# The mixers of block 1: mLSTM gate rows broadcast through DRAM, its scores as three products of two alternating heads, and k norms taken from the transposed k

## The chip, the core and the metric

The kernel runs on one core of a Trainium2 chip. The core has a matrix engine (TensorE, in the profile PE, with its weight loads as PEld), a vector engine (VectorE, DVE), a scalar engine (ScalarE, ACT), a general engine (GpSimd, POOL) and queues that start DMA transfers (one is SyncE's, SP; GpSimd and ScalarE have their own). Each engine takes its instructions in the order in which they stand in its queue, and a wait of the first holds all behind it. The metric is the device time of one execution in microseconds (us), as a median over runs.

## The reference

The program is a two-block transformer in float32 with one sequence of T = 512 rows and a width of 1024. The change lies in the two recurrent mixers of block 1. Both have H = 4 heads. What they compute, cut to what matters here:

```python
# gated delta rule: q, k, v after a causal convolution of width 4 and silu, heads of 128
q = _l2norm(q) * (dk ** -0.5)          # _l2norm(x) = x * rsqrt(sum(x*x, -1) + 1e-6)
k = _l2norm(k)
# mLSTM: q, k with 64 per head, v with 128; b = running sum of log sigmoid(f_pre)
d_log = where(incl, b[..., :, None] - b[..., None, :] + i[..., None, :], -inf)
s = einsum('bhcd,bhsd->bhcs', q_i, k_i) * exp(d_log - m_t[..., None])
num = ... + einsum('bhcs,bhse->bhce', s, v_i)
den = ... + sum(s, axis=-1)
h = num / maximum(abs(den), exp(-m_t))[..., None]
```

The kernel computes the mLSTM in one piece over all 512 rows: per head a triangle of scores between key block j and all later queries, each score times the exponential of a row term (one number a query, the same for all keys of a block) plus a column term.

## The kernel before

**The large products.** Nearly all of the work is products of a weight slab (1024x128) with the 512 columns of the activations. A slab is loaded by SP (raw, 512 KB), cast to its leading part by ACT (`whi`, line 101), and the rest is subtracted by DVE (`wlo`, line 102). Then PE multiplies three times for each of 8 pieces: 24 matmuls of 128x512 in the reduced format fp32r, lines 173 to 175.

**Who sets the order.** PE's order in block 1 is written out by hand. The slab products stand in a list, `todo`, cut into steps of six matmuls (four steps a slab). The code of the mixers is written between calls of `fill(n)`, which issue n such steps. A slab that is done may hand work over for later: `after(n, fn)` runs `fn` once n more steps are issued.

```python
def after(n, fn):
    late.append((now[0] + n, fn))
def fill(n):
    for _ in range(n):
        run_late(now[0])
        now[0] += 1
        while todo and next(todo[0], 1):
            todo.pop(0)
```

The order of all other engines is set by a scheduler when the program is built; at run time it is fixed.

**The delta rule's k.** When the slab of a head's k is done, `k_done` runs: a convolution and silu on DVE and ACT (`conv_silu`: `cx`, four operations on `ac`, `kt`), then six steps later `g`. There PE sums the squares of k by four matmuls against a column of ones (`l2cols`, `pc`, line 474) and transposes k into `pk` (line 490). DVE adds a constant to the sums (`rqk`), GpSimd raises them to the power -1/2, and DVE multiplies `pk` by them into `kn` (line 491). Two steps later `g2` transposes `kn` back (`pk2`, line 497; the trace calls its tile pk too). The list has k, q and v of each of the four heads in turn.

**The mLSTM.** Row terms `rj` (4 heads x 1280: the triangle's four blocks of 512, 384, 256 and 128 queries, one after the other) are made on 4 partitions. `enm` (line 582) is an exponential of the transposed running maximum `pm`. Then, head after head and for each of the four j: one float32 product over 64 rows, `psS` (line 592, two records in the trace); two products that spread the row terms to 128 partitions, `psr` (line 596); the exponential on ACT (`D`, line 598); a mask on GpSimd; the product of `psS` and `D` on DVE (`Sm`, line 601); `fill(2)`. After the four j come `psn` (line 608) in two parts, each with `fill(2)` behind it, copies of its columns on ACT and its last columns into `den` on DVE. `pm`, `psr`, `psS` and `psn` share one ring of two PSUM tiles, tag `sa`.

Of the kernel before, what the change touches and what calls it, by code (L numbers as in the profile page):

```python
# [21 lines left out]
FFT = 22
EPS = 1e-6
# [30 lines left out]
def block_kernel(ctx: ExitStack, tc: tile.TileContext, xT, pT, cols, cst, wA, wBr, wO, w13, w2, wPG, wPL,  # L54
                 aIn, aRI, aO, bQKV, bO, f13, f2, outT, dbg=None, upto=99):
    nc = tc.nc
    V, S, G, TE = nc.vector, nc.scalar, nc.gpsimd, nc.tensor

    def dump(name, aps):
        if dbg and name in dbg:  # L60
            for i, a in enumerate(aps):
                nc.sync.dma_start(dbg[name][i], a)
# [133 lines left out]
    def bc_in(ap, n):  # L196
        return ap.unsqueeze(2).to_broadcast([ap.shape[0], ap.shape[1], n])
# [4 lines left out]
    def pw(out, in_):  # L202
        G.tensor_tensor(out, in_, mhalf[:, :in_.shape[1]], op=ALU.pow)
# [47 lines left out]
    def xtile(k):  # L251
        return xp.tile([P, T], F32, tag=f"x{k}", name=f"x{k}")
# [35 lines left out]
    with ExitStack() as ca:  # L288
# [47 lines left out]
        psk = [gemm(pmm, wA[O_MK], A)]  # L336
# [5 lines left out]
        psq0 = gemm(pps, wA[O_MQ], A, tag="sb")  # L342
        R = norm_rows(pn, "nr", ss, "R0", rc0)
        LB = ca.enter_context(tc.tile_pool(name="LB", bufs=1, reuse_waits="tile"))
        o_b = LB.tile([P, H, T], F32, name="o_b")
        gz = LB.tile([P, H, T], F32, name="gz")
        cg = ExitStack()
        GP = cg.enter_context(tc.tile_pool(name="GP", bufs=1, reuse_waits="tile"))
# [11 lines left out]
        V.tensor_tensor(zr, psg, R, op=ALU.mult)  # L360
        V.tensor_scalar(zr, zr, col("gbias"), None, op0=ALU.add)

        mkT, mqT = [xtile(0), xtile(1)], [xtile(2), xtile(3)]
        for i in range(2):
            V.tensor_tensor(mkT[i], psk[i], R, op=ALU.mult)
        mv = ML.tile([P, NB, H, P + 1], F32, name="mv")
        G.memset(mv[:, :, :, P:P + 1], 1.0)

        def mq_done(i):
            return lambda ps: V.scalar_tensor_tensor(mqT[i], ps, 0.125, R, op0=ALU.mult, op1=ALU.mult)  # L370

        def mv_done(h):
            def f(ps):
# [92 lines left out]
        def l2sq(src):  # L466
            sq = CV.tile([P, T], F32, tag="sq", bufs=2, name="sqk")
            S.activation(sq, src, AF.Square)
            return sq

        def l2cols(sq, which, h):
            pc = pn.tile([P, NB], F32, tag="nr", name="pc")
            for b in range(NB):
                TE.matmul(pc[:, b:b + 1], sq[:, b * P:(b + 1) * P], onec, start=True, stop=True)
            r = rqk[:, which, h, :]
            V.tensor_scalar(r, pc, EPS, None, op0=ALU.add)
            pw(r, r)
            return r

        def k_done(h):  # L480
            def f(ps):
                kt = CV.tile([P, T], F32, tag="cv", bufs=3, name="kt")
                conv_silu(ps, 3 * h, kt)
                sq = l2sq(kt)

                def g():
                    rk = l2cols(sq, 0, h)
                    pk = pt("pk", "sb")
                    for b in range(NB):
# [40 lines left out]
        def mo_done(h):  # L530
            def f(ps):
                assert ob_ready
                th = tp.tile([P, T], F32, tag="xin", bufs=3, name="tho")
                V.tensor_tensor(th, ps, R, op=ALU.mult)
                S.activation(th, th, AF.Tanh, scale=0.5)
                V.tensor_scalar(th, th, 0.5, 0.5, op0=ALU.mult, op1=ALU.add)
                V.tensor_tensor(o_b[:, h, :], o_b[:, h, :], th, op=ALU.mult)
            return f

        LAG = 6  # L540
# [22 lines left out]
        ro = (0, 512, 896, 1152)  # L563
# [4 lines left out]
            V.tensor_scalar(rj[:, ro[j] + P:ro[j + 1]], rj[:, ro[j + 1]:ro[j + 1] + T - (j + 1) * P],  # L568
                            rows[:, 2, (j + 1) * P - 1:(j + 1) * P], None, op0=ALU.add)
        fill(8)  # L570
        sel = ML.tile([H, H], F32R, name="sel")
        V.tensor_copy(sel, ident[0:H, 0:H])
        rjh = ML.tile([H, 1280], F32R, name="rjh")
        S.copy(rjh, rj)
        V.tensor_tensor(rj, rj, rjh.bitcast(F32), op=ALU.subtract)
        rjl = ML.tile([H, 3 * T], F32R, tag="rows", name="rjl")[:, 0:1280]
        V.tensor_copy(rjl, rj)
        pm = pt("pm", shape=(P, NB, H))
        for b in range(NB):
            TE.transpose(pm[:, b, :], mrow[:, b * P:(b + 1) * P], ident[0:H, 0:H])  # L580
# [2 lines left out]
        num = [xtile(4 + b).rearrange("p (h d) -> p h d", h=H) for b in range(NB)]  # L583
        den = ML.tile([P, NB, H], F32, name="den")
        msq = ML.tile([P, NB, H], F32, name="msq")
        for h in range(H):
            p0 = (h % 2) * 64
            Sm = ML.tile([P, 1280], F32, tag="Sm", bufs=1, name="Sm")
            for j in range(NB):
                w = T - j * P  # L590
                psS = pt("psS", shape=(P, T))
                TE.matmul(psS[:, 0:w], mkT[h // 2][p0:p0 + 64, j * P:(j + 1) * P], mqT[h // 2][p0:p0 + 64, j * P:],
                          start=True, stop=True)
                psr = pt("psr", shape=(P, T))
                for n, r_ in enumerate((rjl, rjh)):
                    TE.matmul(psr[:, 0:w], sel[:, h:h + 1].to_broadcast([H, P]), r_[:, ro[j]:ro[j] + w], start=(n == 0), stop=(n == 1))
                D = ML.tile([P, T], F32, tag="D", bufs=2, name="D")
                S.activation(D[:, 0:w], psr[:, 0:w], AF.Exp, bias=ccol[:, j, h:h + 1])
                G.affine_select(D[:, 0:P], D[:, 0:P], pattern=[[1, P]], base=0, channel_multiplier=-1,
                                compare_op=ALU.is_ge, fill=0.0)  # L600
                V.tensor_tensor(Sm[:, ro[j]:ro[j] + w], psS[:, 0:w], D[:, 0:w], op=ALU.mult)
                fill(2)
            for i2 in range(2):
                psn = pt("psn", shape=(P, 2, P + 1))
                for ii in range(2):
                    i = 2 * i2 + ii
                    for j in range(i + 1):
                        TE.matmul(psn[:, ii, :], Sm[:, ro[j] + (i - j) * P:ro[j] + (i - j + 1) * P], mv[:, j, h, :], start=(j == 0), stop=(j == i))
                for ii in range(2):
                    S.copy(num[2 * i2 + ii][:, h, :], psn[:, ii, 0:P])  # L610
                V.tensor_copy(den[:, 2 * i2:2 * i2 + 2, h:h + 1], psn[:, :, P:P + 1])
                fill(2)
# [791 lines left out]
```

## Time and profile before

| what | value |
|---|---|
| median of 3 runs | 2080.74 us (2080.17 to 2080.78) |
| profiled execution, its own time | 2082.17 us |
| span of that execution, first to last instruction | 2080.2 us |
| busy: PE / DVE / ACT / POOL | 2051.9 / 1104.5 / 763.9 / 257.1 us |
| mean granted TensorE clock | 0.995 |

The busy times are of the same span. PE lacks 28 us of it, the others far more. The mixers' code that the change touches runs from about 60 to 180 us; each head's turn takes some 27.5 us there.

### The profile page before, as it was taken

The page shows a single profiled execution, that of the slowest core. Times are in us where ns is not written, and L with a number is a line of the kernel's source. Part 1 is how long each engine was busy: PE and PEld are TensorE (multiplying, and loading weights), DVE is VectorE, ACT ScalarE, POOL GpSimd, SP SyncE. Part 2 cuts the span into 40 slices and gives each one's busy share as a digit, 9 for nine tenths or more (in the row PEclk, how much of TensorE's full clock was granted, in tenths as well). Part 3 has the DMA queues.
Part 4 walks back from the last instruction along what each step waited for, and adds up shares of the span by engine and source line. Part 5 has one row for each costly group of instructions (what it writes and reads, how often), then busy time and mean ns, then how long its engine had stood idle before and what let it go on. Part 6 is the DMA issues. An engine that isn't in the chain of part 4 may idle for free.

```text
span 2080.2 us, 24373 instructions
## 1 busy us (share of the span) xinstructions
PE 2051.9 (99%) x9786; PEld 1705.2 (82%) x9786; DVE 1104.5 (53%) x1455; ACT 763.9 (37%) x1099; POOL 257.1 (12%) x266
## 2 busy tenths in 40 slices
PE   8999999999999999999899999999999999999998
PEld 7778899888888888887788888888888888888887
DVE  5667453554444423669964444333877754444322
ACT  4334232333232322546642323223555533322221
POOL 0111000131000000252320000001322220000011
PEclk9999999999999999999999999999999999999999
DMA  4211111343333333322323333333122123333332
GB/s 168 71 55 59 60 41 43 105 127 101 97 96 100 91 97 98 114 79 82 91 91 96 97 101 92 92 101 98 55 61 72 41 77 96 91 102 94 92 102 68
DMA packets 53664, 181.69 MB, mean 87 GB/s; under 512 B 5808, under 2 KB 7984, under 8 KB 53552
## 3 DMA queue, kind: packets, MB, share of 16 engines
q1 hardware_dynamic: 53408, 180.05, 28.9%
q8 instruction: 76, 1.25, 0.3%
q14 instruction: 36, 0.29, 0.0%
q10 hardware_dynamic: 144, 0.10, 0.0%
HBM read 178.03 MB, written 2.10 MB: 87 GB/s over the span
## 4 chain that ended last, share of the span: by engine, by line
PE 91%; DVE 5%; ACT 1%; issue 1%; POOL 1%; DMA 1%; SPq 0%; POOLq 0%; DVEq 0%; ACTq 0%
PE psmm L173 19%; PE psmm L174 19%; PE psmm L175 19%; PE psd L173 6%; PE psd L175 6%; PE psd L174 6%; PE z L1119 2%; PE po L1157 1%; DVE wlo L102 1%; PE pU L731 1%; PE pX L726 1%; PE t L1146 1%; DVE xc L987 1%; PE psv L173 1%; PE psv L174 1%
## 5 line engine op out<-in xcount | busy, mean ns | idle before, releaser
L101 ACT CAST whi<-raw 128x1024 fp32r<-128x1024 f32 (+1 forms) x333 | 344.5, 1036 | 942.3 <-issue 374.5
L102 DVE TENSOR_TENSOR wlo<-raw,whi 128x1024 fp32r<-128x1024 f32 (+1 forms) x333 | 411.0, 1235 | 287.9 <-ACT whi L101 287.8
L173 PE MATMUL psmm<-Bh,wlo 128*128 128x512 f32 x1032 | 402.3, 390 | 0.3 <-DVE Ol L1162 0.3
L174 PE MATMUL psmm<-Bl,whi 128*128 128x512 f32 x1032 | 402.2, 390 | 0.1
L175 PE MATMUL psmm<-Bh,whi 128*128 128x512 f32 x1032 | 402.1, 390 | 0.0
L173 PE MATMUL psmm<-Ah,wlo 128*128 128x512 f32 x832 | 332.9, 401 | 2.8 <-DVE wlo L102 1.9
L175 PE MATMUL psmm<-Ah,whi 128*128 128x512 f32 x832 | 325.2, 391 | 0.0
L174 PE MATMUL psmm<-Al,whi 128*128 128x512 f32 x832 | 324.4, 390 | 0.6 <-DVE Al L189 0.6
L173 PEld LDWEIGHTS psmm<-Bh,wlo 128*128 128x128 f32 x1032 | 193.8, 188 | 40.8 <-DVE Ol L1162 0.5
L175 PEld LDWEIGHTS psmm<-Bh,whi 128*128 128x128 f32 x1032 | 193.8, 188 | 40.3
L174 PEld LDWEIGHTS psmm<-Bl,whi 128*128 128x128 f32 x1032 | 193.8, 188 | 40.2 <-DVE Bl L189 0.5
L216 POOL TENSOR_TENSOR ss<-ss,sq 128x512 f32<-128x512 f32 x55 | 85.6, 1561 | 1141.7 <-issue 803.7
L173 PE MATMUL psd<-Hh,wlo 128*128 128x512 f32 x506 | 196.8, 389 | 0.0
L174 PE MATMUL psd<-Hl,whi 128*128 128x512 f32 x506 | 196.8, 389 | 0.0
L175 PE MATMUL psd<-Hh,whi 128*128 128x512 f32 x506 | 196.8, 389 | 0.0
L173 PEld LDWEIGHTS psmm<-Ah,wlo 128*128 128x128 f32 x832 | 156.3, 188 | 36.0 <-DVE wlo L102 3.2
L175 PEld LDWEIGHTS psmm<-Ah,whi 128*128 128x128 f32 x832 | 156.1, 188 | 33.6
L174 PEld LDWEIGHTS psmm<-Al,whi 128*128 128x128 f32 x832 | 156.6, 188 | 30.3 <-DVE Al L189 1.1
L870 DVE TENSOR_TENSOR u<-psmm,R 128x512 f32<-128x512 f32 x66 | 45.6, 691 | 194.2 <-PE psmm L175 194.2
L866 DVE TENSOR_TENSOR s<-psmm,R 128x512 f32<-128x512 f32 x66 | 45.7, 692 | 137.0 <-PE psmm L175 134.0
L175 PEld LDWEIGHTS psd<-Hh,whi 128*128 128x128 f32 x506 | 95.0, 188 | 19.8
L174 PEld LDWEIGHTS psd<-Hl,whi 128*128 128x128 f32 x506 | 95.0, 188 | 19.8
(468 smaller groups left out, 2475.9 us busy)
## 6 DMA issues: line engine op xcount, KB each, us to landing
raw<-in_f SPq DMA_DIRECT2D x120, 512.0 KB, 3.6
raw<-in_w SPq DMA_DIRECT2D x60, 512.0 KB, 3.5
raw<-in_wA SPq DMA_DIRECT2D x43, 512.0 KB, 3.5
raw<-in_bQKV SPq DMA_DIRECT2D x24, 512.0 KB, 3.5
raw<-in_aIn SPq DMA_DIRECT2D x16, 512.0 KB, 3.6
raw<-in_f SPq DMA_DIRECT2D x16, 384.0 KB, 3.1
x<-in_xT SPq DMA_DIRECT2D x16, 256.0 KB, 3.6
raw<-in_wBr SPq DMA_DIRECT2D x8, 512.0 KB, 3.5
```

The costliest lines, as they stand in the source:

```text
L101: copied[0] = S.copy(hi[:, :nk, :], raw[:, :nk, :])
L102: V.tensor_tensor(lo[:, :nk, :], raw[:, :nk, :], hi[:, :nk, :].bitcast(F32), op=ALU.subtract)
L173: TE.matmul(ps, l, xh, start=(first and i == 0), stop=False)
L174: TE.matmul(ps, h, xl, start=False, stop=False)
L175: TE.matmul(ps, h, xh, start=False, stop=(last and i == n - 1))
L216: eng.tensor_tensor(self.acc, self.acc, sq, op=ALU.add)
L726: heads(lambda h: TE.matmul(pX[:, h], Nm[:, h, :], odd(U)[:, h], start=True, stop=True))
L731: heads(lambda h: TE.matmul(pU[:, h], Tt[:, h, :], X[:, h], start=True, stop=True))
L866: V.tensor_tensor(s1, p1, R, op=ALU.mult)
L870: V.tensor_tensor(u, p3, R, op=ALU.mult)
L987: V.scalar_tensor_tensor(ac, cx[:, j:j + T], col("aconv", 4 * k + j), ac, op0=ALU.mult, op1=ALU.add)
L1119: TE.matmul(zs[g][:, o:o + w], qp[a][qs], kp[b][p0:p0 + 64, 0:w], start=(n == 0 and o == 0), stop=(n == 2), skip_group_check=True)
```

## The change

It has three parts. **Rows:** `rj` is written to DRAM by a DMA of GpSimd's queue, and read back for each head with every row spread over 128 partitions, into `Sm` tiles of 128x1280 (655 KB each, three of them); heads 0 and 1 ahead of the loop, 2 and 3 at the start of its second half. The exponential and the mask work in place there. **Scores:** k and q of the mLSTM are split into a leading part and a rest, and the scores are three fp32r products over 64 rows instead of one float32 product; two heads take turns, one on rows 0 to 63 and one on rows 64 to 127. The loop over j now serves two heads and has `fill(4)`; the `psn` parts of both heads follow. **k norms:** PE's four matmuls of sums are gone; the transposes come first, ACT squares `pk`, and DVE sums the squares by a reduction along the free axis. `g2` still comes two steps after `g`.

Left out of the diff: `mlo`, the tile of the rests, shares its place with `o_b`, which is made later and so becomes a list; the tile of squares `sqm` has one buffer instead of two.

```diff
         V.tensor_scalar(zr, zr, col("gbias"), None, op0=ALU.add)
-        mkT, mqT = [xtile(0), xtile(1)], [xtile(2), xtile(3)]
-        for i in range(2):
-            V.tensor_tensor(mkT[i], psk[i], R, op=ALU.mult)
+        def mparts(k, src, c):
+            t = ML.tile([P, T], F32, tag="mvt", bufs=2, name="mkq")
+            V.scalar_tensor_tensor(t, src, c, R, op0=ALU.mult, op1=ALU.mult)
+            pair = xp.tile([P, T], F32R, tag=f"x{k}", name=f"mh{k}"), mlo[:, k, :]
+            split(pair, t)
+            return pair
+        mkT, mqT = [mparts(i, psk[i], 1.0) for i in range(2)], [None, None]
         mv = ML.tile([P, NB, H, P + 1], F32, name="mv")
         G.memset(mv[:, :, :, P:P + 1], 1.0)
         def mq_done(i):
-            return lambda ps: V.scalar_tensor_tensor(mqT[i], ps, 0.125, R, op0=ALU.mult, op1=ALU.mult)
+            return lambda ps: mqT.__setitem__(i, mparts(2 + i, ps, 0.125))
         def mv_done(h):
             def f(ps):
...
             def f(ps):
                 kt = CV.tile([P, T], F32, tag="cv", bufs=3, name="kt")
                 conv_silu(ps, 3 * h, kt)
-                sq = l2sq(kt)
                 def g():
-                    rk = l2cols(sq, 0, h)
                     pk = pt("pk", "sb")
                     for b in range(NB):
                         TE.transpose(pk[:, b, :], kt[:, b * P:(b + 1) * P], ident)
+                    sq = CV.tile([P, NB, P], F32, tag="sq", bufs=2, name="sqk")
+                    S.activation(sq, pk, AF.Square)
+                    rk = rqk[:, 0, h, :]
+                    V.tensor_reduce(rk, sq, axis=AX.X, op=ALU.add)
+                    V.tensor_scalar(rk, rk, EPS, None, op0=ALU.add)
+                    pw(rk, rk)
                     V.tensor_tensor(kn[:, :, h, :], pk, bc_in(rk, P), op=ALU.mult)
                     after(2, g2)
...
             V.tensor_scalar(rj[:, ro[j] + P:ro[j + 1]], rj[:, ro[j + 1]:ro[j + 1] + T - (j + 1) * P],
                             rows[:, 2, (j + 1) * P - 1:(j + 1) * P], None, op0=ALU.add)
         fill(8)
-        sel = ML.tile([H, H], F32R, name="sel")
-        V.tensor_copy(sel, ident[0:H, 0:H])
-        rjh = ML.tile([H, 1280], F32R, name="rjh")
-        S.copy(rjh, rj)
-        V.tensor_tensor(rj, rj, rjh.bitcast(F32), op=ALU.subtract)
-        rjl = ML.tile([H, 3 * T], F32R, tag="rows", name="rjl")[:, 0:1280]
-        V.tensor_copy(rjl, rj)
+        rjd = dp.tile([H, 1280], F32, name="rjd")
+        G.dma_start(rjd, rj)
+        def rowsbc(h):
+            t = ML.tile([P, 1280], F32, tag="Sm", bufs=3, name="Sm")
+            G.dma_start(t, rjd[h].partition_broadcast(P))
+            return t
+        Sms = [rowsbc(h) for h in range(2)]
         pm = pt("pm", shape=(P, NB, H))
         for b in range(NB):
             TE.transpose(pm[:, b, :], mrow[:, b * P:(b + 1) * P], ident[0:H, 0:H])
...
         num = [xtile(4 + b).rearrange("p (h d) -> p h d", h=H) for b in range(NB)]
         den = ML.tile([P, NB, H], F32, name="den")
         msq = ML.tile([P, NB, H], F32, name="msq")
-        for h in range(H):
-            p0 = (h % 2) * 64
-            Sm = ML.tile([P, 1280], F32, tag="Sm", bufs=1, name="Sm")
+        for hp in range(2):
+            kh, qh = mkT[hp], mqT[hp]
+            if hp:
+                Sms += [rowsbc(h) for h in (2, 3)]
             for j in range(NB):
                 w = T - j * P
-                psS = pt("psS", shape=(P, T))
-                TE.matmul(psS[:, 0:w], mkT[h // 2][p0:p0 + 64, j * P:(j + 1) * P], mqT[h // 2][p0:p0 + 64, j * P:],
-                          start=True, stop=True)
-                psr = pt("psr", shape=(P, T))
-                for n, r_ in enumerate((rjl, rjh)):
-                    TE.matmul(psr[:, 0:w], sel[:, h:h + 1].to_broadcast([H, P]), r_[:, ro[j]:ro[j] + w], start=(n == 0), stop=(n == 1))
-                D = ML.tile([P, T], F32, tag="D", bufs=2, name="D")
-                S.activation(D[:, 0:w], psr[:, 0:w], AF.Exp, bias=ccol[:, j, h:h + 1])
-                G.affine_select(D[:, 0:P], D[:, 0:P], pattern=[[1, P]], base=0, channel_multiplier=-1,
-                                compare_op=ALU.is_ge, fill=0.0)
-                V.tensor_tensor(Sm[:, ro[j]:ro[j] + w], psS[:, 0:w], D[:, 0:w], op=ALU.mult)
-                fill(2)
...
+                psS = [pt("psS", shape=(P, T)) for _ in range(2)]
+                for n, (a, b) in enumerate(((1, 0), (0, 1), (0, 0))):
+                    for c in range(2):
+                        p0 = 64 * c
+                        TE.matmul(psS[c][:, 0:w], kh[a][p0:p0 + 64, j * P:(j + 1) * P], qh[b][p0:p0 + 64, j * P:],
+                                  start=(n == 0), stop=(n == 2))
+                for c in range(2):
+                    h = 2 * hp + c
+                    D = Sms[h][:, ro[j]:ro[j] + w]
+                    S.activation(D, D, AF.Exp, bias=ccol[:, j, h:h + 1])
+                    G.affine_select(D[:, 0:P], D[:, 0:P], pattern=[[1, P]], base=0, channel_multiplier=-1,
+                                    compare_op=ALU.is_ge, fill=0.0)
+                    V.tensor_tensor(D, psS[c][:, 0:w], D, op=ALU.mult)
+                fill(4)
+            for h in (2 * hp, 2 * hp + 1):
+                for i2 in range(2):
...
```

**Place 1: the second transposes of head 0.** In the rows, brackets hold what an instruction has to wait for (an engine, DMASW for a DMA of GpSimd's queue, DMAHW for one of SP's), and a number behind a name is that of its buffer. On PE before stand the last row of a `fill(2)`, the first part of head 0's `psn`, and `pk2`:

```order
L175 MATMUL psmm<-Ah_98,whi 128x512
L608 MATMUL psn<-mv,Sm 128x129 [waits Activation_49]
L608 MATMUL psn<-mv,Sm 128x129 x2
L497 MATMUL pk_835<-CST,kn 128x128 [waits DVE_49]
L497 MATMUL pk_835<-CST,kn 128x128 x3
```

and on DVE the stretch that ends with the multiplication it waits for:

```order
L461 SCALAR_TENSOR_TENSOR ac<-cx,cwh,ac 128x512 [waits DVE_49]
L601 TENSOR_TENSOR Sm<-psS,D 128x256 [waits Pool_49]
L461 SCALAR_TENSOR_TENSOR ac<-cx,cwh,ac 128x512 [waits DVE_49] x2
L601 TENSOR_TENSOR Sm<-psS,D 128x128 [waits PE_49,Pool_49]
L476 TENSOR_SCALAR rqk<-pc 128x4 [waits PE_49]
L464 SCALAR_TENSOR_TENSOR qT<-th,ac 128x512 [waits Activation_49]
L491 TENSOR_TENSOR kn<-pk,rqk 128x4x128 [waits PE_49,Pool_49]
```

On PE now, at the same call of `g2`, after the `psS` of j = 2 (256 columns) of heads 0 and 1:

```order
L176 MATMUL psmm<-Ah_100,whi 128x512
L613 MATMUL psS<-mh_355,mlo 128x256 [waits DVE_49] x2
L613 MATMUL psS<-mlo,mh_343 128x256 x2
L613 MATMUL psS<-mh_355,mh_343 128x256 x2
L510 MATMUL pk_842<-CST,kn 128x128 [waits DVE_49]
L510 MATMUL pk_842<-CST,kn 128x128 x3
L174 MATMUL psmm<-Ah_86,wlo 128x512
```

and on DVE now:

```order
L466 TENSOR_TENSOR cx<-psmm,R_317 128x512 [waits PE_49]
L621 TENSOR_TENSOR Sm<-psS,Sm 128x256 [waits PE_49]
L621 TENSOR_TENSOR Sm<-psS,Sm 128x256 [waits PE_49,Pool_49]
L103 TENSOR_TENSOR wlo<-raw,whi 128x1024 [waits DMAHW1_49,Activation_49]
L468 TENSOR_SCALAR ac<-cx,cwh 128x512 [waits DVE_49,Pool_49]
L501 TENSOR_REDUCE rqk<-sqk 128x4 [waits Activation_49]
L470 SCALAR_TENSOR_TENSOR ac<-cx,cwh,ac 128x512 [waits DVE_49]
L502 TENSOR_SCALAR rqk<-rqk 128x4 [waits DVE_49]
L470 SCALAR_TENSOR_TENSOR ac<-cx,cwh,ac 128x512 [waits DVE_49] x2
L504 TENSOR_TENSOR kn<-pk,rqk 128x4x128 [waits Pool_49]
```

`pk2` now follows `psS` of two heads and not `psn`, and on DVE `kn` stands behind the two `Sm` that wait for this `psS`, behind `wlo` and behind the whole convolution of the next slab.

**Place 2: the first scores.** ACT before, around the copies of `mv`, two casts of slabs and `enm`:

```order
L574 CAST rjh<-rj 4x1280 [waits DVE_49]
L101 CAST whi<-raw 128x1024 [waits DMAHW6_49,PE_49]
L381 COPY mv<-pmv 128x4x128 [waits PE_49]
L101 CAST whi<-raw 128x1024 [waits DMAHW7_49,PE_49,Activation_49]
L582 ACTIVATE enm<-pm 128x16 [waits PE_49]
L598 ACTIVATE D<-psr,ccol 128x512 [waits PE_49]
```

and now:

```order
L618 ACTIVATE Sm<-Sm,ccol 128x512 [waits DMASW1_49,DVE_49]
L618 ACTIVATE Sm<-Sm,ccol 128x384
L390 COPY mv<-pmv 128x4x128 [waits PE_49]
L618 ACTIVATE Sm<-Sm,ccol 128x256
L618 ACTIVATE Sm<-Sm,ccol 128x128
L618 ACTIVATE Sm<-Sm,ccol 128x512 [waits DMASW2_49]
L618 ACTIVATE Sm<-Sm,ccol 128x384
L618 ACTIVATE Sm<-Sm,ccol 128x256
L618 ACTIVATE Sm<-Sm,ccol 128x128
L102 CAST whi<-raw 128x1024 [waits DMAHW7_49,DVE_49,PE_49]
L598 ACTIVATE enm<-pm 128x16 [waits PE_49]
```

`enm`, whose input tile `pm` lies where the second `psS` of the pair is to go, now stands behind the exponentials of heads 0 and 1, and these behind the landing of their DMAs.

**Place 3: the second transposes of head 1.** On PE now:

```order
L176 MATMUL psmm<-Ah_100,whi 128x512
L629 MATMUL psn<-mv,Sm 128x129 [waits DMASW2_49,DVE_49,Pool_49]
L629 MATMUL psn<-mv,Sm 128x129
L629 MATMUL psn<-mv,Sm 128x129 [waits Pool_49]
L510 MATMUL pk_1041<-CST,kn 128x128 [waits DVE_49]
L510 MATMUL pk_1041<-CST,kn 128x128 x3
```

and on DVE now:

```order
L466 TENSOR_TENSOR cx<-psmm,R_317 128x512 [waits PE_49]
L501 TENSOR_REDUCE rqk<-sqk 128x4 [waits Activation_49]
L468 TENSOR_SCALAR ac<-cx,cwh 128x512 [waits DVE_49,Pool_49]
L103 TENSOR_TENSOR wlo<-raw,whi 128x1024 [waits DMAHW4_49,Activation_49]
L502 TENSOR_SCALAR rqk<-rqk 128x4 [waits DVE_49]
L470 SCALAR_TENSOR_TENSOR ac<-cx,cwh,ac 128x512 [waits DVE_49]
L632 COPY den<-psn 128x2 [waits PE_49,Activation_49]
L470 SCALAR_TENSOR_TENSOR ac<-cx,cwh,ac 128x512 [waits DVE_49]
L504 TENSOR_TENSOR kn<-pk,rqk 128x4x128 [waits Pool_49]
```

Here `pk2` follows the first part of head 1's `psn`; `kn` stands behind the copy of that `psn`'s last columns (`den`) and the convolution of the slab that ended just before it.

## Rows read from the trace of the kernel before

**Rows 1.** The page, part 1: busy time of the engines over the whole span.
```profile
PE 2051.9 (99%) x9786; PEld 1705.2 (82%) x9786; DVE 1104.5 (53%) x1455; ACT 763.9 (37%) x1099; POOL 257.1 (12%) x266
```

**Rows 2.** The chain that ended last, 65 to 180 us, by line.
```profile
by line: PE psmm L173 22.6%; PE psmm L175 20.6%; PE psmm L174 20.5%; PE psS L592 10.2%; PE psn L608 7.8%; PE psr L596 6.9%; PE pc L474 6.2%; PE pk L490 1.7%; PE pv L517 1.5%; PE pk L497 1.5%; PE pmv L380 0.4%; PE pm L580 0.3%
```

**Rows 3.** PE in order of time: start us, us, line, operation, operands.
```profile
69.50 1.12 PE L592 MATMUL psS<-x,x 64*128 64x512 f32 x2
...
71.21 0.50 PE L173 MATMUL psmm<-Ah,wlo 128*128 128x512 f32 x1
71.55 0.39 PE L174 MATMUL psmm<-Al,whi 128*128 128x512 f32 x1
71.78 0.39 PE L175 MATMUL psmm<-Ah,whi 128*128 128x512 f32 x1
```

**Rows 4.** PE at the 64-row products of block 2, in order of time.
```profile
1486.80 0.50 PE L1119 MATMUL z<-kl,qh 64*128 64x512 f32 x1
...
1488.14 0.22 PE L1119 MATMUL z<-kl,qh 64*128 64x128 f32 x1
...
1488.43 0.33 PE L1119 MATMUL z<-kl,qh 64*128 64x256 f32 x1
```

**Rows 5.** DVE in order of time, 78 to 87 us (idle time ahead in brackets).
```profile
78.58 0.69 DVE L457 TENSOR_TENSOR cx<-psmm,R 128x512 f32<-128x512 f32 x1 [1.40 <-PE psmm L175]
79.31 0.49 DVE L459 TENSOR_SCALAR ac<-cx,cwh 128x512 f32<-128x512 f32 x1
79.71 1.22 DVE L102 TENSOR_TENSOR wlo<-raw,whi 128x1024 fp32r<-128x1024 f32 x1
80.85 0.78 DVE L461 SCALAR_TENSOR_TENSOR ac<-cx,cwh,ac 128x512 f32<-128x512 f32 x1
81.55 0.41 DVE L601 TENSOR_TENSOR Sm<-psS,D 128x256 f32<-128x256 f32 x1
...
84.34 0.16 DVE L476 TENSOR_SCALAR rqk<-pc 128x4 f32<-128x4 f32 x1
...
86.00 0.69 DVE L491 TENSOR_TENSOR kn<-pk,rqk 128x512 f32<-128x512 f32 x1 [0.90 <-POOL rqk L203]
```

**Rows 6.** PE in order of time, at the second transposes of head 0.
```profile
87.41 0.83 PE L608 MATMUL psn<-mv,Sm 128*128 128x129 f32 x6
88.08 0.60 PE L497 MATMUL pk<-CST,kn 128*128 128x128 f32 x4
```

**Rows 7.** Groups of instructions, 60 to 190 us: busy us, mean ns | idle before.
```profile
L203 POOL TENSOR_TENSOR rqk<-rqk,mhalf 128x4 f32<-128x4 f32 x8 | 9.6, 1194 | 15.1 <-DVE rqk L476 15.1
L598 ACT ACTIVATE D<-psr,ccol 128x512 f32<-128x512 f32 (+3 forms) x16 | 8.5, 529 | 27.1 <-PE psr L596 27.0
L616 DVE TENSOR_REDUCE msq<-sqm 128x4 f32<-128x512 f32 x4 | 2.6, 666 | 0.0
```

**Rows 8.** DVE and then ACT in order of time.
```profile
59.61 1.09 DVE L568 TENSOR_SCALAR rj<-rj,rows 4x128 f32<-4x128 f32 x3
...
69.31 1.04 ACT L101 CAST whi<-raw 128x1024 fp32r<-128x1024 f32 x1 [2.22 <-PE psmm L175]
```

**Rows 9.** DMA issues: queue, count, KB each, median us from issue to landing.
```profile
raw<-in_wA SPq DMA_DIRECT2D x43, 512.0 KB, 3.5
...
CST<-in_cst SPq DMA_DIRECT2D x1, 704.0 KB, 6.3
...
COL<-in_cols ACTq DMA_DIRECT2D x1, 97.0 KB, 3.2
```

**Rows 10.** PE in order of time, around a wait in block 2.
```profile
987.08 0.39 PE L175 MATMUL psmm<-Bh,whi 128*128 128x512 f32 x1
992.16 0.79 PE L173 MATMUL pr<-xch,wlo 128*128 128x512 f32 x1 [4.69 <-DVE wlo L102]
...
998.24 0.39 PE L175 MATMUL pr<-xch,whi 128*128 128x512 f32 x1
```

**Rows 11.** Windows: us, busy time of each engine, granted TensorE clock (PEclk).
```profile
994.00:996.00 2.00, 2.00 (x6) 1.58 (x5) 2.00 (x4) 0.83 (x1) 0.00 (x0) 0.50 0.65 227
```

More of the change, by code (lines that the diff above doesn't have):

```diff
@@ L68, in block_kernel @@
     pn = ctx.enter_context(tc.tile_pool(name="pn", bufs=1, space=PSUM))
+    dp = ctx.enter_context(tc.tile_pool(name="dp", bufs=1, space=bass.MemoryType.DRAM))
     WP = [ctx.enter_context(tc.tile_pool(name="wh2", bufs=2, side="right"))]
@@ L344, in block_kernel @@
         LB = ca.enter_context(tc.tile_pool(name="LB", bufs=1, reuse_waits="tile"))
-        o_b = LB.tile([P, H, T], F32, name="o_b")
+        mlo = LB.tile([P, 4, T], F32R, tag="ob", name="mlo")
+        o_b = []
         gz = LB.tile([P, H, T], F32, name="gz")
@@ L536, in f @@
                 V.tensor_scalar(th, th, 0.5, 0.5, op0=ALU.mult, op1=ALU.add)
-                V.tensor_tensor(o_b[:, h, :], o_b[:, h, :], th, op=ALU.mult)
+                V.tensor_tensor(o_b[0][:, h, :], o_b[0][:, h, :], th, op=ALU.mult)
             return f
@@ L585, in block_kernel @@
         msq = ML.tile([P, NB, H], F32, name="msq")
-        for h in range(H):
-            p0 = (h % 2) * 64
-            Sm = ML.tile([P, 1280], F32, tag="Sm", bufs=1, name="Sm")
+        for hp in range(2):
+            kh, qh = mkT[hp], mqT[hp]
+            if hp:
+                Sms += [rowsbc(h) for h in (2, 3)]
             for j in range(NB):
                 w = T - j * P
-                psS = pt("psS", shape=(P, T))
-                TE.matmul(psS[:, 0:w], mkT[h // 2][p0:p0 + 64, j * P:(j + 1) * P], mqT[h // 2][p0:p0 + 64, j * P:],
-                          start=True, stop=True)
-                psr = pt("psr", shape=(P, T))
-                for n, r_ in enumerate((rjl, rjh)):
-                    TE.matmul(psr[:, 0:w], sel[:, h:h + 1].to_broadcast([H, P]), r_[:, ro[j]:ro[j] + w], start=(n == 0), stop=(n == 1))
-                D = ML.tile([P, T], F32, tag="D", bufs=2, name="D")
-                S.activation(D[:, 0:w], psr[:, 0:w], AF.Exp, bias=ccol[:, j, h:h + 1])
-                G.affine_select(D[:, 0:P], D[:, 0:P], pattern=[[1, P]], base=0, channel_multiplier=-1,
-                                compare_op=ALU.is_ge, fill=0.0)
-                V.tensor_tensor(Sm[:, ro[j]:ro[j] + w], psS[:, 0:w], D[:, 0:w], op=ALU.mult)
-                fill(2)
[L603 to L612, printed above, removed]
@@ new lines, in block_kernel @@
+                fill(4)
+            for h in (2 * hp, 2 * hp + 1):
+                for i2 in range(2):
+                    psn = pt("psn", shape=(P, 2, P + 1))
+                    for ii in range(2):
+                        i = 2 * i2 + ii
+                        for j in range(i + 1):
+                            TE.matmul(psn[:, ii, :], Sms[h][:, ro[j] + (i - j) * P:ro[j] + (i - j + 1) * P], mv[:, j, h, :], start=(j == 0), stop=(j == i))
+                    for ii in range(2):
+                        S.copy(num[2 * i2 + ii][:, h, :], psn[:, ii, 0:P])
+                    V.tensor_copy(den[:, 2 * i2:2 * i2 + 2, h:h + 1], psn[:, :, P:P + 1])
+                    fill(2)
@@ L613, in block_kernel @@
         for b in range(NB):
-            sqm = ML.tile([P, H, P], F32, tag="D", bufs=2, name="sqm")
+            sqm = ML.tile([P, H, P], F32, tag="D", bufs=1, name="sqm")
             S.activation(sqm, num[b], AF.Square)
@@ L630, in ob_out @@
         def ob_out():
+            o_b.append(LB.tile([P, H, T], F32, tag="ob", name="o_b"))
             for h in range(H):
@@ L634, in ob_out @@
                     TE.transpose(po[:, b, :], num[b][:, h, :], ident)
-                S.activation(o_b[:, h, :], po.rearrange("p b t -> p (b t)"), AF.Copy, scale=col("mln", h))
-            dump("o_b", [o_b[:, h, :] for h in range(H)])
+                S.activation(o_b[0][:, h, :], po.rearrange("p b t -> p (b t)"), AF.Copy, scale=col("mln", h))
+            dump("o_b", [o_b[0][:, h, :] for h in range(H)])
             ob_ready.append(1)
@@ L820, in block_kernel @@
         for h in range(H):
-            split(oab[4 + h], o_b[:, h, :])
+            split(oab[4 + h], o_b[0][:, h, :])
         for h in range(H):
```

## The prediction

> **What bounds the kernel now.** I read the page first: PE is busy in 99% of the span, the others in 53% and less [rows 1]. So a microsecond is gained where PE has less to do, and lost where it waits. Then the chain of waits for 65 to 180 us, where the mixers' code lies: every line of it is PE's [rows 2]. In these 115 us nothing but PE's own work counts, and DVE, ACT and GpSimd run ahead of it. Last I read PE and DVE in order of time at the places that the change moves, to see how far ahead.
>
> **What PE loses in work.** The float32 scores (`psS`) hold 10.2% and the spread rows (`psr`) 6.9% of the chain's 115 us, together 19.7 us [rows 2]. The column sums (`pc`) hold 6.2%, 7.1 us, half of it for k: 3.6 us. After a float32 product the first fp32r matmul starts 0.34 us (71.21 to 71.55) and not 0.23 us (71.55 to 71.78) before the next [rows 3]; places with such a change of format go from 16 to 8, which is 0.9 us.
>
> **What PE gains in work.** Three fp32r products over 64 rows are not in these mixers before, but block 2 has them, in the same shapes: the 512 and 384 wide ones take 1.34 us together (1486.80 to 1488.14), the 128 wide ones 0.29 (1488.14 to 1488.43) [rows 4]. The 256 wide ones are followed by something else; half way between their neighbours I estimate 0.41. That is 2.04 us a head, 8.2 us for four. PE's net: -19.7 - 3.6 - 0.9 + 8.2 = -16.0 us.
>
> **The waits for `kn`.** Before, head 0's `kn` ends at 86.69 (86.00 + 0.69) [rows 5] and `pk2` starts at 88.08 [rows 6]: 1.4 us to spare. Now `kn` stands behind work that can't start before the slab ahead of `pk2` is done on PE: DVE's `cx` reads that slab's product. From the slab's end PE has only `psS` (two heads of 256 columns, 2 x 0.41 = 0.8 us) or the first part of `psn` (87.41 to 88.08, 0.67 us [rows 6]) to do, and then needs `kn`.
>
> Head 0, in DVE's new order, durations from [rows 5] and the reduction's from [rows 7]: `cx` 0.69, two `Sm` 0.82, `wlo` 1.22, `ac` 0.49, reduction 0.67, `ac` 0.78, `rqk` 0.16, two `ac` 1.56, `kn` 0.69: 7.08 us. Starts lie some 0.08 closer than these durations (79.71 to 80.85 is 1.14 for 1.22), so ten steps take 0.8 off: 6.3. Less PE's 0.8: a wait of 5.5 us. GpSimd's power takes 1.19 us [rows 7] and is covered by the two `ac` behind it.
>
> Head 1: `cx` 0.69, reduction 0.67, `ac` 0.49, `wlo` 1.22, `rqk` 0.16, `ac` 0.78, `den` (as `rqk`) 0.16, `ac` 0.78, `kn` 0.69: 5.64, less 0.64 for closer starts, less `psn` 0.67: 4.3 us.
>
> Head 2 has head 0's place, with `qT` (0.78, as `ac`) more on DVE: 7.86, less 0.9, less 0.8: 6.2; only one `ac` lies between `rqk` and `kn`, so 0.5 of the power shows: 6.7 us. Head 3 has head 1's place, with a reduction of squares more: 6.31, less 0.7, less 0.67: 4.9 us. The four waits: 5.5 + 4.3 + 6.7 + 4.9 = 21.4 us. DVE's stretch starts with a wait for PE, as `cx` at 78.58 waited 1.40 us for it [rows 5], so DVE can't begin it early, and I take it that it isn't late there already. A bound from below: were `cx` and `Sm` free, 1.5 less at heads 0 and 2 and 0.7 at 1 and 3, 17.0. From above, durations without closer starts: 24.4.
>
> **The wait for the rows.** The second `psS` of the first pair takes the buffer of `pm` and needs `enm`, which on ACT stands behind both heads' exponentials and one `whi`. `rj` is ready at 59.61 + 1.09 = 60.7 [rows 8]. No GpSimd DMA is in the trace before. The write of 20 KB I put at the 3.2 us of the 97 KB load on another queue, the 655 KB reads between the 3.5 us of 512 KB and the 6.3 us of 704 KB [rows 9]. By the former both heads' rows are there at 67.4; eight exponentials of 0.53 [rows 7] end at 71.6, `whi` takes 1.04 [rows 8], `enm` some 0.2: 72.9, and PE wants it at 69.50 [rows 3]: a wait of 3.4 us. By the latter, with the second read 3.5 us behind the first: 73.7, four exponentials 2.1, then 1.2, so 77.0: 7.5 us. I take 4.0, near the short end, since 43 loads took 3.5 us and the 6.3 us are of a single load at the program's start. Below the short end there's the 3.2 us also for the reads: 3.1 us.
>
> The Trainium skill ("DMA: Bandwidth & Descriptors", section "Anatomy of one DMA — SWDGE (gpsimd) path") gives for GpSimd's transfers 2.0 us and a microsecond per 436 KB. By it, as an estimate, a read takes 3.5 us and the sum would be 0.6 us less than by my 4.0. No run here shows such a transfer yet.
>
> **The clock after a wait.** In block 2 PE waited 4.69 us once, to 992.16 [rows 10]. The granted clock behind it was 0.50, the lower level of 1.2 GHz [rows 11], and the 14 matmuls to 998.24 took 6.08 us; at 0.23 each [rows 3] they take 3.2: 2.9 us lost beyond the wait. Three of the new waits are longer than 4.69 (5.5, 6.7, 4.9) and I count 2.9 for each, 8.6 us; the two shorter ones (4.3, 4.0) I count with none. The ends are 0 and 5 x 2.9 = 14.4.
>
> **Edits that I cost at nothing.** Splitting k and q adds four casts on ACT and four subtractions on DVE (0.69 each, as `cx`), ahead of 60 us and one at a time between slabs; ACT and DVE have spare time there. Without that cover it is 2.8 us. The eight exponentials, now in one lump, stand ahead of a `whi`; PE sits behind `enm` on the same queue, so that is in the 4.0 already. The reads for heads 2 and 3 go through GpSimd's queue; the last waits for head 0's `psn`, and four fills and head 1's `psn` lie between that and its use. `o_b` on the place of `mlo` is made after all scores.
>
> **Sum.** -16.0 + 21.4 + 4.0 + 8.6 = +18.0 us. On the profiled execution's 2082.17 that is 2100.2; the median of the runs lies 1.4 us under that execution, so 2098.7, rounded 2099.
>
> **Rivals.** *The clock holds* after waits of this length: one wait in another stretch is a thin base, and there the PE had other work behind it. Then 8.6 us less: 2090.
>
> *The rows come late.* A slab of 24 matmuls at 0.23 us lasts 5.5 us and brings a load of 512 KB, and the three reads may come behind it and behind each other. The first wait becomes 7.5 and takes the clock with it: 3.5 + 2.9 more, 2105; with a wait at head 3's rows of the same kind up to 2111. Against it: such a load lands in 3.5 us [rows 9], so the way is free for part of each slab.
>
> *Two heads side by side.* The products of a pair use different halves of the rows, in turns. If both of a pair ran in the time of one, the scores would cost 4.1 and not 8.2: 2095. No row before has two such products next to each other; for it speaks that they don't share a row, against it that the six 64-row products of block 2 from 1486.80 to 1488.14 take 0.22 us each, as full ones (0.23) do. In "TensorE: Matmul & The Clock Gate", section "Part 3: Packing small matmuls — row/col tiling", the Trainium skill says that matmuls at different row groups run at the same time. By that rule the 4.1 us would be gained; no run here shows it yet.
>
> *`kn` is not late* (the other side). If DVE had `kn` ready at each `pk2`, neither the 21.4 us nor the 8.6 us would be lost: 2099 - 30 = 2069, faster. It decides where the four waits and the clock cost under 16.0 - 4.0 = 12 us in all, some 3 us a wait with the clock held. For it: DVE is idle nearly half of the span, and only 1.4 us early at this place before. Against it: the order has `kn` behind `cx`, `wlo` and three `ac`, and `cx` needs the slab that ends just ahead.
>
> **How the numbers follow.** My forecast (all waits, three of them with the clock) 0.45, by its own terms 2094 to 2104; the clock holds 0.18; rows late 0.16; heads side by side 0.10; `kn` not late 0.07; the terms meet near zero, within 0.2% (4 us, about what a measurement of this kernel can tell from no change), 0.04. The range of 2086 to 2111 leaves out the last two and the tails of the second and third. Faster 0.07, same 0.05, slower 0.88.
>
> **What would show it.** PE's waits by releaser: four waits for DVE's `kn` at `pk2`, of 4 to 7 us, and one for ACT's `enm` at the first `psS`. A granted clock of 0.5 for some microseconds behind the longer ones. PE's chain without `psr`, with `psS` at some 8 us in all. The forecast is wrong if `pk2` follows without a wait (then DVE's order isn't what binds), if `psS` takes half of its time, or if the clock stays at full speed.

## The result and the profile after

The changed kernel takes 2100.98 us (median of 4 runs, 2099.54 to 2101.53) against 2080.56 before: a ratio of 1.0097, 95% interval 1.008 to 1.0115, slower by 20.4 us. The profiled execution took 2099.54 us with a span of 2097.6, 17.4 us more than the span before.

PE has less to do now and yet is later; the page's part 1 of the kernel after, beside [rows 1]:

```profile
PE 2042.2 (97%) x9738; PEld 1703.2 (81%) x9738; DVE 1105.2 (53%) x1460; ACT 764.3 (36%) x1102; POOL 260.8 (12%) x271
```

Among the waits of PE over the whole execution are the two that the prediction named; columns are us in total, times, longest us:

```profile
PE pk L510 <- DVE kn L504: 24.0, 4, 7.4
...
PE psS L613 <- ACT enm L598: 3.9, 1, 3.9
```

PE in order of time, the five waits themselves (the idle time ahead stands in brackets):

```profile
74.56 0.79 PE L613 MATMUL psS<-mh,mlo 64*128 64x512 f32 x1 [3.86 <-ACT enm L598]
96.86 1.12 PE L510 MATMUL pk<-CST,kn 128*128 128x128 f32 x4 [6.10 <-DVE kn L504]
126.40 1.11 PE L510 MATMUL pk<-CST,kn 128*128 128x128 f32 x4 [5.60 <-DVE kn L504]
158.80 1.09 PE L510 MATMUL pk<-CST,kn 128*128 128x128 f32 x4 [7.41 <-DVE kn L504]
188.99 1.12 PE L510 MATMUL pk<-CST,kn 128*128 128x128 f32 x4 [4.89 <-DVE kn L504]
```

Before, `pk2` of head 0 came 1.4 us after its `kn` without a wait [rows 5, 6]. DVE after, in order of time, up to head 0's `kn`:

```profile
89.61 0.69 DVE L473 SCALAR_TENSOR_TENSOR qT<-th,ac 128x512 f32<-128x512 f32 x1 [0.70 <-ACT th L472]
90.25 0.69 DVE L466 TENSOR_TENSOR cx<-psmm,R 128x512 f32<-128x512 f32 x1
90.86 0.75 DVE L621 TENSOR_TENSOR Sm<-psS,Sm 128x256 f32<-128x256 f32 x2
91.52 1.22 DVE L103 TENSOR_TENSOR wlo<-raw,whi 128x1024 fp32r<-128x1024 f32 x1
92.65 0.48 DVE L468 TENSOR_SCALAR ac<-cx,cwh 128x512 f32<-128x512 f32 x1
93.05 0.68 DVE L501 TENSOR_REDUCE rqk<-sqk 128x4 f32<-128x512 f32 x1
93.64 0.74 DVE L470 SCALAR_TENSOR_TENSOR ac<-cx,cwh,ac 128x512 f32<-128x512 f32 x1
94.30 0.16 DVE L502 TENSOR_SCALAR rqk<-rqk 128x4 f32<-128x4 f32 x1
94.42 1.54 DVE L470 SCALAR_TENSOR_TENSOR ac<-cx,cwh,ac 128x512 f32<-128x512 f32 x2
96.11 0.69 DVE L504 TENSOR_TENSOR kn<-pk,rqk 128x512 f32<-128x512 f32 x1 [0.15 <-POOL rqk L204]
```

The chain is the one of the prediction, link by link: from `cx` at 90.25 to the end of `kn` at 96.80 are 6.55 us (6.3 were worked out), without a gap until the power. What the prediction didn't see is on ACT, in order of time:

```profile
88.94 0.63 ACT L472 ACTIVATE th<-ac 128x512 f32<-128x512 f32 x1 [4.46 <-DVE ac L470]
90.29 1.05 ACT L102 CAST whi<-raw 128x1024 fp32r<-128x1024 f32 x1 [0.71 <-PE psmm L176]
91.25 0.63 ACT L477 ACTIVATE sqk<-qT 128x512 f32<-128x512 f32 x1
91.78 0.57 ACT L499 ACTIVATE sqk<-pk 128x512 f32<-128x512 f32 x1
```

The first transposes were done near 87.4, but the square of `pk` ran at 91.78: it stands behind `th`, which waits for DVE, and behind a cast that waits for PE to end a slab. So at head 0 the reduction couldn't have come before 92.35 even if it stood first on DVE.

Behind these waits the granted clock is down. Windows behind the first four, columns as in [rows 11] with DMA share and GB/s at the end (behind the fifth, 190 to 195 us, it is 0.80):

```profile
75.00:80.00 5.00, 5.00 (x15) 3.46 (x14) 3.17 (x5) 1.94 (x5) 1.90 (x5) 0.57 0.31 105
...
95.00:100.00 5.00, 3.14 (x10) 2.69 (x11) 2.22 (x4) 1.22 (x2) 1.18 (x2) 0.52 0.13 53
...
125.00:130.00 5.00, 3.60 (x11) 3.02 (x12) 2.04 (x3) 1.10 (x2) 0.98 (x3) 0.50 0.16 65
...
160.00:165.00 5.00, 5.00 (x16) 3.90 (x15) 0.00 (x0) 0.51 (x1) 0.00 (x0) 0.53 0.00 0
```

And the scores are cheaper than forecast. PE in order of time at the first scores of heads 2 and 3, beside [rows 4]:

```profile
136.87 0.51 PE L613 MATMUL psS<-mh,mlo 64*128 64x512 f32 x2
137.20 0.41 PE L613 MATMUL psS<-mlo,mh 64*128 64x512 f32 x2
137.43 0.41 PE L613 MATMUL psS<-mh,mh 64*128 64x512 f32 x2
137.77 0.50 PE L174 MATMUL psmm<-Ah,wlo 128*128 128x512 f32 x1
```

Six products of 512 columns take 0.90 us (136.87 to 137.77); two products, one of each head, start together, the next two 0.23 to 0.33 us later. That is the time of three: in e6 below, three of one head alone take 0.88 us.

### The profile page after: what moved, and what is told of

It is laid out like the page before. It is cut to its first block, busy times and chain, and to the rows that moved or that the text cites. A ratio compares the mean times of both kernels' runs of the same rounds, so it can differ in the third digit from the quotient of the medians.

```text
span 2097.6 us, 24303 instructions
## 1 busy us (share of the span) xinstructions
PE 2042.2 (97%) x9738; PEld 1703.2 (81%) x9738; DVE 1105.2 (53%) x1460; ACT 764.3 (36%) x1102; POOL 260.8 (12%) x271
## 4 chain that ended last, share of the span: by engine, by line
PE 87%; DVE 7%; issue 2%; DMA 1%; ACT 1%; POOL 1%; POOLq 0%; DVEq 0%; ACTq 0%
PE psmm L174 18%; PE psmm L175 18%; PE psmm L176 18%; PE psd L175 5%; PE psd L176 5%; PE psd L174 5%; DVE wlo L103 2%; PE z L1141 1%; PE po L1179 1%; DVE xc L1009 1%; PE pU L753 1%; PE pX L748 1%; PE t L1168 1%; PE psv L174 1%; PE psv L175 1%
## 5 line engine op out<-in xcount | busy, mean ns | idle before, releaser
L174 PEld LDWEIGHTS psd<-Hh,wlo 128*128 128x128 f32 x506 | 95.0, 188 | 19.9
```

The source lines that it names most:

```text
L174: TE.matmul(ps, l, xh, start=(first and i == 0), stop=False)
```

## The experiments

**e1: `g2` six steps after `g`.** Changed kernel with

```diff
-                    after(2, g2)
+                    after(6, g2)
```

> The changed kernel with one number changed: the second transposes of k come six steps after the first, not two. Theory (kn is late on DVE by its place in the order, and each long wait takes some microseconds at half clock with it): the four waits at the second transposes fall from 24.0 us to under 2 us in all, the half-rate stretches behind them go, the wait of 3.9 us for enm stays; 2101 - 24 - 9 = 2068 us. Rival (DVE is short of time in this stretch, whatever is asked of it first): the waits reappear at the next place that needs DVE (psS of 128 columns, pv, psn), and the time stays above 2092.

Measured: 2070.29 us, ratio 0.9953 (0.9937 to 0.997). Waits of PE in the mixers, 31 to 420 us:

```profile
PE psS L613 <- ACT enm L598: 3.9, 1, 3.9
PE pk L510 <- DVE kn L504: 1.0, 1, 1.0
```

One number turns 20 us slower into 10 us faster than before. The waits don't come back elsewhere, and the granted clock from 80 to 200 us is 1.00: DVE isn't short of time there, its `kn` is only late for a fixed place in PE's order. The theory holds, the rival falls.

**e2: the k norms undone.** Changed kernel with

```diff
                 conv_silu(ps, 3 * h, kt)
+                sq = l2sq(kt)
                 def g():
+                    rk = l2cols(sq, 0, h)
                     pk = pt("pk", "sb")
...
-                    S.activation(sq, pk, AF.Square)
-                    rk = rqk[:, 0, h, :]
-                    V.tensor_reduce(rk, sq, axis=AX.X, op=ALU.add)
```

> The changed kernel with the k norms as before (squares on ACT from the untransposed k, four matmuls for the sums), rows and scores as changed. Theory (the chain transposes, square, reduction, power, kn is longer than the two steps, and so kn is set behind the next slab's work): kn stands ahead of the next cx again, no wait at the second transposes; 2101 - 24 - 9 + 4 for the column sums = 2072 us. Rival (the grouping of two heads loads DVE at that place, whatever the norms): waits of 3 us or more stay at heads 0 and 2, 2085 or more.

Measured: 2073.46 us, ratio 0.9968 (0.9955 to 0.9981); the only long wait of the mixers is 3.6 us for `enm`. DVE of this kernel, in order of time, at head 0:

```profile
87.18 0.15 DVE L485 TENSOR_SCALAR rqk<-pc 128x4 f32<-128x4 f32 x1
...
89.00 0.69 DVE L500 TENSOR_TENSOR kn<-pk,rqk 128x512 f32<-128x512 f32 x1 [0.95 <-POOL rqk L204]
...
90.22 0.69 DVE L466 TENSOR_TENSOR cx<-psmm,R 128x512 f32<-128x512 f32 x1
```

With the sums from PE, `kn` stands ahead of the next slab's `cx` and ends at 89.7. The pairing of heads alone makes no wait there.

**e3: the k norms alone.** The kernel before with the opposite edit, and nothing else of the change.

> The kernel before with the k norms alone changed. Theory: kn stands behind cx, reduction, wlo and two others of the next slab, PE waits some 3.6 us at each of the four second transposes (14 us), saves 3.6 us of column sums, and loses 0 to 8 us by the clock: 2091 to 2099, taken 2094. Rival (it needs the grouping of heads too): no such wait, 2077.

Measured: 2103.19 us, ratio 1.0108 (1.0093 to 1.0123). PE's waits for `kn`, 31 to 420 us:

```profile
PE pk L501 <- DVE kn L495: 16.2, 4, 4.3
```

This part alone costs 22.7 us, more than the whole change, and lies above the 2091 to 2099 that were expected. The wait is there without the grouping of heads, so the rival falls. The waits are 1.8 us more than four of 3.6. The span grew by 21.7 us; less 16.2 of waits, plus 3.6 of column sums saved, 9.1 us are left for the clock, above the 8 that were allowed.

**e4: the rows alone.** The kernel before, with `sel`, `rjh`, `rjl` and `psr` gone, and

```diff
+        rjd = dp.tile([H, 1280], F32, name="rjd")
+        G.dma_start(rjd, rj)
+        def rowsbc(h):
+            t = ML.tile([P, 1280], F32, tag="Sm", bufs=2, name="Sm")
+            G.dma_start(t, rjd[h].partition_broadcast(P))
+            return t
+        Sms = [rowsbc(h) for h in range(2)]
...
+                if i2 and h < 2:
+                    Sms.append(rowsbc(h + 2))
```

> The kernel before with the rows alone through DRAM (two Sm tiles, the next head's rows read when a head's psn is done), scores in float32 and heads one after the other. Theory: 7.9 us of psr gone from PE; the buffer of pm is now wanted by the second psS and not the first, so the wait for enm is 1 us or less: 2073 us. Rival (the reads through DRAM are what is slow, for each head): a wait of 2 us or more at each head's first scores or psn, 2082 or more.

Measured: 2072.9 us, ratio 0.9965 (0.9953 to 0.9977), with no wait over 0.8 us in the mixers. The rows through DRAM gain 7.6 us, near the 7.9 of `psr`. `enm` runs about as late as in the changed kernel (73.89 and 74.33), but here the second `psS`, which takes the buffer of `pm`, comes twelve matmuls behind the first, at 74.06.

**e5: e1, and `pm` in the other ring.**

```diff
-        pm = pt("pm", shape=(P, NB, H))
+        pm = pt("pm", "sb", shape=(P, NB, H))
```

> The changed kernel with the second transposes six steps later and pm in the other ring of PSUM tiles, so that the second psS doesn't wait for enm. Theory: the wait of 3.9 us and its half-rate stretch (2.9 us) go as well: 2070.3 - 3.9 - 2.9 = 2063.5 us. Rival (what is late is the rows themselves, by their DMA and the eight exponentials): the wait moves to the second psS pair, which needs the first products with the rows; 2067 us or more.

Measured: 2066.11 us, ratio 0.993 (0.9918 to 0.9942), faster than both kernels. The wait for `enm` is gone and didn't move to the next pair: the theory's mechanism. The gain over e1 is 4.2 us and not 6.8, and why it is less stays open. The two profiled executions differ by only 1.6 us. In them e5 waits 1.0 us more for `kn` (2.0 for 1.0) and 1.9 us more for `wlo` (4.5 for 2.6, over the whole kernel; 2.85 of it at 1019.77 in block 2, which the edit doesn't touch), and behind a wait of 1.40 us in block 2 its granted clock is 0.50 (1640 to 1642) where that of e1 is 1.00 (1643 to 1645).

**e6: e1 with the products of one head ahead of the other's.**

```diff
-                for n, (a, b) in enumerate(((1, 0), (0, 1), (0, 0))):
-                    for c in range(2):
+                for c in range(2):
+                    for n, (a, b) in enumerate(((1, 0), (0, 1), (0, 0))):
```

> The changed kernel with the second transposes six steps later (as e1), and the three products of one head issued ahead of the three of the other, no longer in turns. Theory from the trace after (six products of 512 columns of two heads took 0.90 us in turns, where block 2's pace would give 1.4): it is the turns that let two products run at once; the eight pairs then cost some 2.5 to 3 us more, 2073 us. Rival (different halves of the rows overlap in any order, or the pace is that of 64-row products as such): within 1 us of e1's 2070.3, and the six products keep their 0.9 us.

Measured: 2066.11 us, ratio 0.9932 (0.9919 to 0.9946). My theory falls; the time is also more than 1 us below e1's, which the rival didn't expect. PE in order of time, 512 columns of heads 2 and 3:

```profile
117.41 0.51 PE L613 MATMUL psS<-mh,mlo 64*128 64x512 f32 x2
117.75 0.41 PE L613 MATMUL psS<-mlo,mh 64*128 64x512 f32 x2
117.97 0.42 PE L613 MATMUL psS<-mh,mh 64*128 64x512 f32 x2
118.32 0.66 PE L510 MATMUL pk<-CST,kn 128*128 128x128 f32 x4
```

Issued three and three, the products still run in pairs, in 0.91 us. At the first pair the second head's products had to wait for a buffer, and so ran alone:

```profile
71.65 0.49 PE L613 MATMUL psS<-mh,mlo 64*128 64x512 f32 x1 [0.84 <-DVE Sm L621]
71.98 0.39 PE L613 MATMUL psS<-mlo,mh 64*128 64x512 f32 x1
72.21 0.39 PE L613 MATMUL psS<-mh,mh 64*128 64x512 f32 x1
72.53 0.50 PE L174 MATMUL psmm<-Ah,wlo 128*128 128x512 f32 x1
```

Three products alone take 0.88 us (71.65 to 72.53), as long as six on the two halves. It is the halves of the rows that count, not the turns. The 4 us gained over e1 go with another effect of the same edit: the first pair's second `psS` waits 0.84 us for the multiplication that frees the buffer of the first, where e1 waited 3.87 us for `enm`.

**e7: `g2` four steps after `g`.** As e1, with `after(4, g2)`.

> The changed kernel with the second transposes four steps after the first. They then stand 2.75 us and the column sums of q (0.8 us) later on PE, while kn keeps its place on DVE: waits of some 2.5, 0.5, 3.8 and 0 us are left of 6.1, 5.6, 7.4 and 4.9. Theory (only waits longer than 4.69 us drop the clock, as the prediction counted): no half-rate stretch behind them, 2068 to 2070 + 6.8 = 2077 us. Rival (the clock drops after shorter ones too): half-rate stretches behind the 2.5 or the 3.8 us, 2079 to 2083.

Measured: 2080.3 us, ratio 0.9996 (0.9986 to 1.0005). The waits for `kn` are 2.30, 0.50 and 3.95 us, 6.7 in all, as expected. PE at head 0, and windows behind the three waits, in order of time:

```profile
95.70 1.11 PE L510 MATMUL pk<-CST,kn 128*128 128x128 f32 x4 [2.30 <-DVE kn L504]
```

```profile
96.00:98.00 2.00, 2.00 (x8) 1.71 (x7) 0.50 (x1) 0.59 (x1) 0.00 (x0) 0.50 0.00 0
...
124.00:126.00 2.00, 2.00 (x10) 1.67 (x9) 0.69 (x1) 0.82 (x2) 0.85 (x1) 1.00 0.00 0
149.00:151.00 2.00, 2.00 (x7) 1.71 (x7) 0.00 (x0) 0.59 (x1) 0.00 (x0) 0.50 0.00 0
```

The granted clock is 0.50 behind the waits of 2.30 and 3.95 us and 1.00 behind the one of 0.50. The rival holds: waits far shorter than 4.69 us are followed by half clock too.

## Why the prediction was right, point by point

**The forecast's sum against the trace.** The first `pR` of the next stage starts at 187.59 before and at 207.51 after; 0.70 of that is there before the changed code begins (`psR`, 30.31 and 31.01). So the mixers lose 19.2 us, where +18.0 was predicted. The 1.2 us between them are what the misses leave: the waits +2.6, the wait for `enm` -0.1, the clock +1.6, the scores -2.9. The waits stand where the prediction put them and for its reason; that the misses nearly cancel is luck.

- *The four waits for `kn`*: 5.5, 4.3, 6.7, 4.9, in all 21.4 predicted; 6.10, 5.60, 7.41, 4.89, in all 24.0 measured. The mechanism is shown by e1, e2 and e3. Head 1's forecast was 1.3 us too short, most of it since GpSimd's power took 1.5 us behind the reduction and not 1.19, and at head 1 nothing was put in for it; DVE stood idle 0.93 us for it there, and 0.90 at head 2, where 0.5 was put in:

```profile
125.65 0.69 DVE L504 TENSOR_TENSOR kn<-pk,rqk 128x512 f32<-128x512 f32 x1 [0.93 <-POOL rqk L204]
```

- *The wait for `enm`*: 4.0 predicted, 3.86 measured, and e5 shows that it is the buffer of `pm`. The pieces were off both ways: the write took 2.5 us (3.2 assumed), the first read 4.7 (3.5).
- *PE's work*: the `psr` and half of the `pc` went as counted; -7.9 and -3.6. The scores were mis-sized: 8.2 us were put in for four heads. The pairs of 512 and 384 columns took 0.90 and 0.72 (143.92 to 144.64), that of 256 columns in e1 0.55 (90.54 to 91.09), that of 128 columns 0.48 (105.20 to 105.68). That is 2.65 us a pair of heads and 5.3 for both. PE's net is some -19 and not -16. The rival "two heads side by side" was right as a mechanism, with 2.9 us instead of its 4.1: the forecast's sum had two products of a pair one after the other, and they ran at once. By the rule of the Trainium skill that it cited ("TensorE: Matmul & The Clock Gate", "Part 3: Packing small matmuls — row/col tiling"), products at different row groups run at the same time; the trace agrees, 0.90 us for six products at the pace of three.
- *The clock*: 8.6 us predicted, and 19.2 + 19 - 27.9 leaves some 10 us. The starts of all matmuls from 60 to 210 us give the same: some 7.5 us over the pace of 0.229 in `psmm`, 1.6 in `pk2` (3.0 for 1.4) and 1.2 in the first `psS` (2.1 busy for 0.90). The size is near by luck, the rule behind it was wrong: I let three waits above 4.69 us count with 2.9 us each, and half clock stood behind all five, the one of 3.86 us among them, with some 2 us each; e7 has it behind 2.30 us. The rival "the clock holds" is out.

**From 19.2 to 20.4.** With the 0.70 us from before, the profiled execution after is 19.9 us behind at `pR`, and 17.4 at the end. It gets these 2.5 us back in block 2. There the same wait of 1.40 us for `Ol` stands in both kernels, at a distance of 20.25 us (1652.57 and 1672.82). Behind it the clock was at half in the execution before, and not in the one after. Window of before, then the wait and a window of after:

```profile
1654.00:1656.00 2.00, 2.00 (x9) 1.90 (x8) 0.88 (x2) 1.27 (x2) 0.36 (x2) 0.50 0.00 0
```

```profile
1672.82 0.66 PE L1204 MATMUL pv<-CST,qk 128*128 128x128 f32 x4 [1.40 <-DVE Ol L1184]
```

```profile
1674.00:1676.00 2.00, 2.00 (x15) 1.81 (x14) 1.13 (x2) 1.62 (x4) 0.48 (x2) 1.00 0.00 0
```

The medians are 20.4 us apart because the profiled execution before took 1.6 us more than its median and the one after 1.4 less. The other runs of the changed kernel are 1.0 to 2.0 us slower than the profiled one; that this place is the reason was not shown.

**Where the gain of each part went.** Rows alone gain 7.6 us (e4). Rows and scores together gain 7.0 (e2): the 3.6 us for `enm` and the clock behind it take back a large part of what the lighter scores save; the rest is not accounted for. The k norms save 3.6 us of PE and cost 22.7 net as they stand (e3). With `g2` later and `pm` elsewhere, all three gain 15.2 us (e5).

**What the working left out.** I priced `kn`'s delay by DVE's order alone. The square's place on ACT, behind a cast that waits for the slab's end, holds the reduction back too, but at heads 0 and 2 only. At head 1 the square was done at 119.80, before `cx` could start at 120.17, and stood ahead of the cast:

```profile
119.22 0.58 ACT L499 ACTIVATE sqk<-pk 128x512 f32<-128x512 f32 x1
120.22 1.05 ACT L102 CAST whi<-raw 128x1024 fp32r<-128x1024 f32 x1 [0.42 <-ACT sqk L499]
```

So it was at head 3 (183.10 against 183.46) and at all heads of e3 (86.63 against 87.18 at head 0), and PE waited 3.9 to 5.6 us there as well. DVE's order is enough for such a wait; what ACT's place adds at heads 0 and 2 was not tried.

## What to carry to other kernels

When a hand-written order gives a result a fixed number of steps to arrive, a change that makes its chain longer must move the place where the result is used as well: four columns' sums on PE were 0.9 us a head, and the wait that replaced them 4 to 7. Read the order of the helping engines from the point where they are last held up (here the end of a slab), add the durations up to the operand, and compare with what PE has left to do. And check what shares a buffer with an operand whose producer you have put behind a transfer.

## What the runs showed of the hardware

Two 64-row products on different halves of the rows ran at once, 0.23 us a pair of 512 columns, even where three of one head were issued ahead of three of the other (e6). Six took 0.90 us in pairs and three alone 0.88.

The cost of a PE wait is not its length. In the mixers of the changed kernel half clock added some 10 us to 27.9 us of waits. It followed each of the waits of 3.86 us and more there, in e7 those of 2.30 and 3.95, and in block 2 of the changed kernel a wait of 2.00 for `wlo` that ended at 1055.19. Behind the 1.40 us for `Ol` it stood in six of the nine profiled executions, and in three not (the changed kernel, e1 and e6). Behind the 2.85 us of e5 the clock stayed at 1.00, as it did behind 2.74 to 2.84 us at the same place in e2, e3, e4 and e7. Windows of the changed kernel and of e5:

```profile
1056.00:1058.00 2.00, 2.00 (x6) 1.61 (x5) 1.97 (x2) 0.22 (x1) 1.75 (x1) 0.50 0.84 231
```

```profile
1020.00:1022.00 2.00, 2.00 (x10) 1.62 (x10) 1.97 (x3) 0.00 (x0) 1.87 (x1) 1.00 0.62 147
```

So a single length that decides can't be read from these runs.

A 20 KB write to DRAM from GpSimd's queue landed in 2.5 us and four reads of 640 KB, three of them issued together, in a median of 5.5 (DMA issues of the kernel after; the chain of waits has the first at 4.71):

```profile
Sm<-rjd POOLq DMA_DIRECT2D x4, 640.0 KB, 5.5
...
rjd<-rj POOLq DMA_DIRECT2D x1, 20.0 KB, 2.5
```

```profile
64.48 4.71 DMA Sm<-rjd
```

The figure of a page in the Trainium skill ("DMA: Bandwidth & Descriptors", "Anatomy of one DMA — SWDGE (gpsimd) path") gave an estimate of 3.5 us for such a read; here the measured 4.7 us decides.
